# At three seams of a two-layer trunk, lower parts of two token tiles move from GpSimd to VectorE, tanh's table is loaded at the seam, and VectorE's modulation sums are issued behind their unit

## The chip, the cores and the metric

The kernel runs on one core of a Trainium2 chip. The metric is the device time of one execution, in microseconds (us); of several executions the median counts.

The engines are named as the profile names them: PE (TensorE, matmuls) with PEld (its weight loads), DVE (VectorE), ACT (ScalarE), POOL (GpSimd) and SP (SyncE, which issues most DMAs).

## The reference, cut to what matters

Two layers, each a token mixer and a gated FFN with a width-3 depthwise convolution, on 384 tokens (128 context tokens and 256 latent ones) of width 1024. Each half of a layer normalises its input, modulates it by vectors computed from a condition, and adds its normalised, gated output to the residual stream:

```python
D_MODEL, DEPTH, SEQ, DEC_SEQ, D_FF = 1024, 2, 128, 256, 2816

def modulation(cond, w, b):
    m = jax.nn.silu(cond) @ w + b
    return jnp.split(m[..., None, :], 6, axis=-1)

def conv_ffn(h, p):
    gate, up = jnp.split(h @ p['ffn_w_up'], 2, axis=-1)
    gate = dwconv3(gate, p['ffn_conv_w'], p['ffn_conv_b'])
    return (jax.nn.silu(gate) * up) @ p['ffn_w_down']

def trunk_layer(x, mod, p, cache):
    shift1, scale1, gate1, shift2, scale2, gate2 = mod
    h = rms_norm(x, p['norm_g'][0]) * (1.0 + scale1) + shift1
    y, ctx_state = token_mixer(h, p, cache)
    x = x + gate1 * rms_norm(y, p['norm_g'][1])
    h = rms_norm(x, p['norm_g'][2]) * (1.0 + scale2) + shift2
    x = x + gate2 * rms_norm(conv_ffn(h, p), p['norm_g'][3])
    return x, ctx_state
```

Everything is float32.

## The kernel before

**Tiles and products.** The 384 tokens are three tiles of 128 (0, 1, 2). A float32 product is three matmuls: each operand is split into an upper part (a rounding cast) and a lower part (what is left). For weights ACT casts the upper part (`whi`, line 358) and DVE subtracts the lower part (`wlo`, line 359). The input of a projection lies transposed in `hTa` and `hTb` (the two halves of its 1024 columns), each in an upper and a lower part. The upper part is ACT's cast in line 815, the lower part a subtraction in line 818. Line 818 goes to POOL by default, and to DVE in the variants `La` and `Lv`.

**Seams.** Between two halves of a layer stands a seam: for each token tile the post-norm, the residual, the pre-norm, transposes, modulation and split, while PE finishes the last product before and starts the first one behind. The steps of a seam are issued in an order written out by hand, as a string of names; the function `in_order` calls them one by one, and each engine runs its own in that order. There are three such strings that matter here: `OUT_ORDER` (layer 0, mixer to FFN; about 262 to 290 us, called seam A), `FFN_ORDER` (FFN of layer 0 to mixer of layer 1; about 560 to 590 us, seam B) and `OUT_LAST_ORDER` (layer 1, mixer to FFN; about 770 to 798 us, seam C).

A name is a step and a tile number. Those that come up below, `a` and `v` being the halves that ACT and DVE work on:

- `x`: the residual (line 779, DVE); `z`: the normalised tile `xn` (`za` on ACT, line 797; `zv` on DVE, line 795); `t`: its transposes on PE into `tps` (line 802); `h`: the modulation of `tps` into `hf` (`ha` on ACT, line 812; `hv` on DVE, line 810); `i`: the upper part (line 815); `l`: the lower part on POOL, `L` with `a` or `v`: the lower part on DVE (line 818).
- `g`, `u`, `G`, `U`: matmuls of the first FFN unit's gate (`gps`) and up half (`ups`): small letters are the columns of the first two tiles (up to column 258 in layer 0), capitals those behind. `k` is the like for the first projection of layer 1 (`tma`, lines 878 to 880).
- `L` and `A` with a number: load and matmuls of a part of the next layer's modulation (`adaps`, line 407). `W`: eight idle matmuls. `m`: matmuls of the product before the seam.

**The FFN loop.** It runs over 22 units of 128 hidden columns, f = 0 to 21, ordered by a scheduler. A unit is the gate product (24 matmuls of 386 columns into `gps`), a step of the down product (18 matmuls of 512 columns into `facc`, lines 1302 to 1304, for the unit before), and the up product (24 matmuls into `ups`). `gate_act` (line 1311) does the convolution and the activation: line 1315 on ACT, 1316 and 1317 on DVE, tanh in line 1318 on ACT, 1319 on DVE. Line 1562 multiplies by `ups`; the result is split into `fah` (ACT) and `fal` (DVE), the stationary operands of the next unit's down step.

**Modulation sums.** In the FFN of layer 0, half of layer 1's modulation is computed on DVE: `AdaV.rows` (line 501) loads 512 KB blocks into `avr` (two buffers) and adds four products for each pair of blocks into `avc` (lines 503 and 505). The loop advances this by one pair of blocks in unit 3 and in each unit from 6 on. The scheduler puts the sums in DVE's queue where it sees room.

Of the kernel before, what the change touches and what calls it, by code (L numbers as in the profile page):

```python
# [9 lines left out]
F32 = mybir.dt.float32  # L10
# [3 lines left out]
ACTF = mybir.ActivationFunctionType  # L14
ALU = mybir.AluOpType
# [7 lines left out]
TP = 386  # L23
# [245 lines left out]
def trunk(ctx: ExitStack, tc: tile.TileContext, A, O, offs, depth=DEPTH):  # L269
    nc = tc.nc  # L270
    coff0, coff, foff, poff, moff = offs
    V, S, G, T = nc.vector, nc.scalar, nc.gpsimd, nc.tensor
# [211 lines left out]
    class AdaV(Ada):  # L484
# [900 lines left out]
    for l in range(depth):  # L1385
# [147 lines left out]
        with ExitStack() as ph:  # L1533
# [8 lines left out]
            for f in range(NF):  # L1542
# [44 lines left out]
            steps, more = [{} for _ in range(3)], {}  # L1587
# [60 lines left out]
```

## Time and profile before

| | before |
|---|---|
| median of 3 runs | 1080.4 us |
| the three runs | 1078.41, 1080.73, 1080.4 us |
| the profiled execution | 1076.9 us |
| its span | 1075.1 us |
| mean granted TensorE clock | 0.994 |
| PE busy | 1048.2 us, 97% of the span |
| DVE busy | 735.1 us, 68% |
| ACT busy | 512.8 us, 48% |
| POOL busy | 65.9 us, 6% |

The median and the three runs are executions without a profile; the span is the profiled execution's own. The granted clock is a share of full speed, 1.00 being 2.4 GHz and 0.50 being 1.2 GHz. Each row of a timeline gives the start and the length of an instruction in us, its engine and line, what it writes and reads, and in brackets how long its engine stood idle before it and which instruction ended that.

### The profile page before, as it was taken

How to read it: one execution, taken by the hardware profiler on the slowest of the kernel's cores; microseconds unless marked ns; L12 is line 12 of the kernel's file. 1: busy time of each engine (PE TensorE's matmuls, PEld its weight loads, DVE VectorE, ACT ScalarE, POOL GpSimd, SP SyncE). 2: the span in 40 equal slices, each digit the busy share in tenths (PEclk: the TensorE clock that was granted, in tenths of full speed). 3: DMA queues.
4: the chain of work that ended last, by engine and by line, in shares of the span. 5: the costliest groups of instructions: out<-in, count | busy, mean ns of one | idle time of the engine just before them, and what ended most of it. 6: DMA issues, size and time to landing. Idle time of an engine off the chain costs nothing.

```text
span 1075.1 us, 15668 instructions
## 1 busy us (share of the span) xinstructions
PE 1048.2 (97%) x5763; PEld 894.4 (83%) x5763; DVE 735.1 (68%) x1554; ACT 512.8 (48%) x1120; POOL 65.9 (6%) x78
## 2 busy tenths in 40 slices
PE   9999999999889999999998999999999999999997
PEld 3497777768789999989986978977899999999996
DVE  6887875576789984489957677757665455445544
ACT  5765545435744433333446554553674434334333
POOL 3210001000200000000003000101020000000000
PEclk9999999999999999999999999999989999999999
DMA  9774455747557764357656522321545334343301
GB/s 345 238 273 135 154 180 216 289 134 277 179 195 246 235 197 140 121 176 234 209 154 212 196 66 73 98 65 49 207 138 177 118 118 132 127 133 119 121 18 59
DMA packets 53305, 176.05 MB, mean 164 GB/s; under 512 B 8650, under 2 KB 10570, under 8 KB 52973
## 3 DMA queue, kind: packets, MB, share of 16 engines
q1 hardware_dynamic: 49517, 171.19, 47.6%
q10 hardware_dynamic: 3712, 3.87, 1.0%
q8 instruction: 45, 0.74, 0.3%
q14 instruction: 31, 0.25, 0.1%
HBM read 169.60 MB, written 5.44 MB: 163 GB/s over the span
## 4 chain that ended last, share of the span: by engine, by line
PE 86%; DVE 8%; DMA 3%; ACT 2%; issue 1%; POOL 0%; DVEq 0%; SPq 0%; ACTq 0%; POOLq 0%
PE facc L1302 6%; PE facc L1304 6%; PE gps L383 6%; PE facc L1303 6%; PE gps L385 6%; PE gps L384 6%; PE ups L383 5%; PE ups L385 5%; PE ups L384 5%; PE fmps L383 3%; PE fmps L385 3%; PE fmps L384 3%; PE acc L1302 2%; PE acc L1303 2%; PE acc L1304 2%; PE adaps L407 2%
## 5 line engine op out<-in xcount | busy, mean ns | idle before, releaser
L359 DVE TENSOR_TENSOR wlo<-raw,whi 128x512 fp32r<-128x512 f32 (+2 forms) x388 | 254.2, 684 | 162.9 <-ACT whi L358 162.1
L358 ACT CAST whi<-raw 128x512 fp32r<-128x512 f32 (+2 forms) x388 | 221.1, 610 | 260.9 <-DMA raw<-in_wdn_dram 98.1
L1302 PE MATMUL facc<-whi,fah 128*128 128x512 f32 x264 | 105.1, 398 | 2.7 <-ACT fah L358 2.7
L1304 PE MATMUL facc<-whi,fal 128*128 128x512 f32 x264 | 104.8, 398 | 0.0
L1303 PE MATMUL facc<-wlo,fah 128*128 128x512 f32 x264 | 104.5, 396 | 0.0
L505 DVE SCALAR_TENSOR_TENSOR avc<-avr,cs,avc 128x1024 f32<-128x1024 f32 x56 | 70.2, 1280 | 0.2 <-DMA avr<-in_ada_dram 0.2
L383 PE MATMUL gps<-hTa,whi 128*128 128x386 f32 (+4 forms) x184 | 62.4, 339 | 0.2 <-DVE fc L1317 0.2
L383 PE MATMUL gps<-hTb,whi 128*128 128x386 f32 (+4 forms) x184 | 62.2, 338 | 0.0
L383 PE MATMUL ups<-hTa,whi 128*128 128x386 f32 (+4 forms) x184 | 62.2, 338 | 0.0
L383 PE MATMUL ups<-hTb,whi 128*128 128x386 f32 (+4 forms) x184 | 61.6, 335 | 0.6 <-ACT hTb L815 0.6
L384 PE MATMUL ups<-hTb,whi 128*128 128x386 f32 (+4 forms) x184 | 61.4, 334 | 0.8 <-POOL hTb L818 0.8
L385 PE MATMUL gps<-hTa,wlo 128*128 128x386 f32 (+4 forms) x184 | 62.1, 338 | 0.0
L385 PE MATMUL ups<-hTa,wlo 128*128 128x386 f32 (+4 forms) x184 | 61.9, 337 | 0.0
L384 PE MATMUL ups<-hTa,whi 128*128 128x386 f32 (+4 forms) x184 | 61.8, 336 | 0.0
L384 PE MATMUL gps<-hTa,whi 128*128 128x386 f32 (+4 forms) x184 | 61.8, 336 | 0.0
L385 PE MATMUL gps<-hTb,wlo 128*128 128x386 f32 (+4 forms) x184 | 61.7, 335 | 0.0
L384 PE MATMUL gps<-hTb,whi 128*128 128x386 f32 (+4 forms) x184 | 61.7, 335 | 0.0
L385 PE MATMUL ups<-hTb,wlo 128*128 128x386 f32 (+4 forms) x184 | 61.5, 334 | 0.0
L1302 PEld LDWEIGHTS facc<-whi,fah 128*128 128x128 f32 x264 | 49.8, 189 | 13.9 <-ACT fah L358 3.0
L1304 PEld LDWEIGHTS facc<-whi,fal 128*128 128x128 f32 x264 | 50.1, 190 | 12.0
L1303 PEld LDWEIGHTS facc<-wlo,fah 128*128 128x128 f32 x264 | 50.0, 190 | 10.1
L1318 ACT ACTIVATE fth<-fc 128x386 f32<-128x386 f32 x44 | 23.2, 528 | 58.5 <-DVE fc L1317 58.4
(392 smaller groups left out, 2392.6 us busy)
## 6 DMA issues: line engine op xcount, KB each, us to landing
raw<-in_wup_dram SPq DMA_DIRECT2D x88, 512.0 KB, 3.8
araw<-in_ada_dram SPq DMA_DIRECT2D x64, 512.0 KB, 4.5
raw<-in_wdn_dram SPq DMA_DIRECT2D x44, 512.0 KB, 3.8
avr<-in_ada_dram SPq DMA_DIRECT2D x32, 512.0 KB, 4.6
raw<-in_win_dram SPq DMA_DIRECT2D x30, 512.0 KB, 3.9
raw<-in_wout_dram SPq DMA_DIRECT2D x16, 512.0 KB, 3.7
gg<-gd SPq DMA_DIRECT2D x8, 512.0 KB
raw<-in_wta_dram SPq DMA_DIRECT2D x8, 416.0 KB, 3.4
```

The lines of the kernel that those rows point to most:

```text
L358: S.copy(hi, src)
L359: (eng or V).tensor_tensor(out=lo, in0=src, in1=hi, op=ALU.subtract)
L383: T.matmul(out, ah, bh, start=start, stop=False)
L384: T.matmul(out, ah, bl, start=False, stop=False)
L385: T.matmul(out, al, bh, start=False, stop=stop)
L407: T.matmul(self.ps[32 * j:32 * j + 32, :], cs[:, k, :], rows[j // 2][:, 512 * (j % 2):512 * (j % 2) + 512], start=(k == self.k0), stop=(k ...
L505: V.scalar_tensor_tensor(out=acc[:, v, c], in0=raw, scalar=sc, in1=acc[:, v, c], op0=ALU.mult, op1=ALU.add)
L1302: T.matmul(acc[t][h], ah[:, cs_], wh_[:, hs], start=first, stop=False)
L1303: T.matmul(acc[t][h], ah[:, cs_], wl_[:, hs], start=False, stop=False)
L1304: T.matmul(acc[t][h], al[:, cs_], wh_[:, hs], start=False, stop=last)
L1318: S.activation(out=th, in_=c, func=ACTF.Tanh)
```

## The change

1. In `OUT_ORDER` and `OUT_LAST_ORDER` the four lower parts `lv1`, `la1`, `lv2`, `la2` become `Lv1`, `La1`, `Lv2`, `La2`: the same subtraction on DVE. In `FFN_ORDER` the same four move to DVE and to other places: `La1 Lv1` behind `zv2`, and `Lv2 La2` behind `W0`. The lower parts of tile 0 stay on POOL.
2. A new step `th` behind `ia2` in `OUT_ORDER` and `OUT_LAST_ORDER`: a tanh of one column on ACT, which makes ACT load the table of tanh there.
3. `AdaV.rows` issues its sums behind the multiplication of line 1562 of the unit at hand.

```diff
@@ OUT_ORDER, from ia0 on @@
-n2 iv1 L3 ya2 A0 ia0 lv1 ha1 xa2 xb2 sa2 A1 sb2 c2 A2 R2 u0 P2 N2 zv2 g0 ia1 za2 la0 A3 tv2 hv2 ta2 iv2 la1 g1
-ha2 lv2 ia2 W0 u1 U0 hold la2  G0 G1 U1 
+L3 ya2 A0 ia0 Lv1 ha1 xa2 xb2 sa2 A1 sb2 c2 A2 R2 u0 P2 N2 zv2 g0 ia1 za2 la0 A3 tv2 hv2 ta2 iv2 La1 g1 ha2 Lv2
+ia2 th W0 u1 U0 hold La2 G0 G1 U1
@@ OUT_LAST_ORDER, from xa2 on @@
-xa2 lv0 hv1 sa2 c2 R2 W2 P2 ia0 N2 za2 iv1 u0 zv2 ta1 g0 ha1 tv2 ta2 la0 g1 hv2 u1 iv2 lv1 ia1 ha2 lv2 la1 ia2
-la2 G0 W3 U0 U1 G1
+lv0 hv1 sa2 c2 R2 W2 P2 ia0 N2 za2 iv1 u0 zv2 ta1 g0 ha1 tv2 ta2 la0 g1 hv2 u1 iv2 Lv1 ia1 ha2 Lv2 La1 ia2 th
+La2 G0 W3 U0 U1 G1
@@ FFN_ORDER, its end @@
-iv0 yb2 n2 xa2 xb2 lv0 ha1 sa2 sb2 c2 R2 A2 hv1 ia1 P2 iv1 N2 la1 k0 zv2 za2 tv2 ta2 ha2 hv2 iv2 ia2 L3 A3 lv1
- k1 W0 lv2 la2 k2 as
+yb2 n2 xa2 xb2 lv0 ha1 sa2 sb2 c2 R2 A2 hv1 ia1 P2 iv1 N2 k0 zv2 La1 Lv1 za2 tv2 ta2 ha2 hv2 iv2 ia2 L3 A3 k1 W0
+Lv2 La2 k2 as
@@ new function @@
+    def tanh_table():
+        y = sm.tile([128, 1], F32, tag="sqt", name="tht")
+        S.activation(out=y, in_=zero8[:, 0:1], func=ACTF.Tanh)
@@ AdaV.rows @@
-                    for v in range(2):
-                        sc = cs[:, k, v:v + 1]
-                        if k == 0:
-                            V.tensor_scalar(acc[:, v, c], raw, sc, None, ALU.mult)
-                        else:
-                            V.scalar_tensor_tensor(out=acc[:, v, c], in0=raw, scalar=sc, in1=acc[:, v, c], op0=ALU.mult, op1=ALU.add)
+
+                    with tc.issue_after(unit[0].ins):
+                        for v in range(2):
+                            sc = cs[:, k, v:v + 1]
+                            if k == 0:
+                                V.tensor_scalar(acc[:, v, c], raw, sc, None, ALU.mult)
+                            else:
+                                V.scalar_tensor_tensor(out=acc[:, v, c], in0=raw, scalar=sc, in1=acc[:, v, c], op0=ALU.mult,
+                                                       op1=ALU.add)
@@ the seam's steps, and the FFN loop @@
+            more["th"] = tanh_table
...
-                V.tensor_tensor(out=c, in0=pu[:, 0:TP], in1=c, op=ALU.mult)
+                unit[0] = V.tensor_tensor(out=c, in0=pu[:, 0:TP], in1=c, op=ALU.mult)
```

DVE at seam A, before: from the last `yn` (line 774) to the first weight splits of the FFN. Names are what an instruction writes and reads.

```order
L774 TENSOR_TENSOR yn<-acc,gg 128x512
L779 SCALAR_TENSOR_TENSOR x_2653<-yn,rz,x_2653 128x512 x2
...
L795 TENSOR_SCALAR xn<-x_2653,rz 128x512
L810 TENSOR_SCALAR hf<-tps,vec_2209,vec_1947 128x128 x4
L416 COPY sb<-adaps 128x512
L359 TENSOR_TENSOR wlo<-raw,whi 128x512 x6
```

The same place now (line 774 is 781, 779 is 786, 795 is 802, 810 is 817, 818 is 825):

```order
L781 TENSOR_TENSOR yn<-acc,gg 128x512
L825 TENSOR_TENSOR hTb<-hf,hTb 128x4x128
L786 SCALAR_TENSOR_TENSOR x_2653<-yn,rz,x_2653 128x512 x2
...
L802 TENSOR_SCALAR xn<-x_2653,rz 128x512
L817 TENSOR_SCALAR hf<-tps,vec_2209,vec_1947 128x128 x4
L825 TENSOR_TENSOR hTa<-hf,hTa 128x4x128
L825 TENSOR_TENSOR hTb<-hf,hTb 128x4x128
L420 COPY sb<-adaps 128x512
L825 TENSOR_TENSOR hTa<-hf,hTa 128x4x128
L363 TENSOR_TENSOR wlo<-raw,whi 128x512 x6
```

Four subtractions are in DVE's queue that were in POOL's: `Lv1` ahead of tile 2's residual, `La1` and `Lv2` behind the modulation `hv2`, `La2` ahead of the weight splits.

DVE at the start of layer 0's FFN, before: from the gate convolution of unit 0 to the split of its result.

```order
L1316 SCALAR_TENSOR_TENSOR fc<-gps,ffh,fc 128x385
L359 TENSOR_TENSOR wlo<-raw,whi 128x512
L1317 SCALAR_TENSOR_TENSOR fc<-gps,ffh,fc 128x385
L359 TENSOR_TENSOR wlo<-raw,whi 128x512 x3
L503 TENSOR_SCALAR avc<-avr,cs 128x1024
L1319 SCALAR_TENSOR_TENSOR fc<-fth,fc 128x386
L1316 SCALAR_TENSOR_TENSOR fc<-gps,ffh,fc 128x385
L1562 TENSOR_TENSOR fc<-ups,fc 128x386
L1317 SCALAR_TENSOR_TENSOR fc<-gps,ffh,fc 128x385
L359 TENSOR_TENSOR wlo<-raw,whi 128x512
L359 TENSOR_TENSOR fal<-fc,fah 128x386
```

The same place now (1316 is 1323, 1317 is 1324, 1319 is 1326, 1562 is 1571, 359 is 363):

```order
L1323 SCALAR_TENSOR_TENSOR fc<-gps,ffh,fc 128x385
L363 TENSOR_TENSOR wlo<-raw,whi 128x512
L1324 SCALAR_TENSOR_TENSOR fc<-gps,ffh,fc 128x385
L363 TENSOR_TENSOR wlo<-raw,whi 128x512 x2
L1326 SCALAR_TENSOR_TENSOR fc<-fth,fc 128x386
L363 TENSOR_TENSOR wlo<-raw,whi 128x512
L1571 TENSOR_TENSOR fc<-ups,fc 128x386
L363 TENSOR_TENSOR wlo<-raw,whi 128x512
L1323 SCALAR_TENSOR_TENSOR fc<-gps,ffh,fc 128x385
L363 TENSOR_TENSOR fal<-fc,fah 128x386
```

The sum of line 503 is gone from between the weight splits and unit 0's `fc`; the first sums now stand behind line 1571 of unit 3.

PE at the first down step (`facc`), before: the rows ahead of it are the second half of unit 1's up product.

```order
L383 MATMUL ups<-hTb,whi 128x386
L384 MATMUL ups<-hTb,whi 128x386
L385 MATMUL ups<-hTb,wlo 128x386
L383 MATMUL ups<-hTb,whi 128x386
L384 MATMUL ups<-hTb,whi 128x386
L385 MATMUL ups<-hTb,wlo 128x386
L1302 MATMUL facc<-whi,fah 128x512
```

The same place now (383 is 387, 385 is 389, 1302 is 1309):

```order
L387 MATMUL ups<-hTa,whi 128x386
L388 MATMUL ups<-hTa,whi 128x386
L389 MATMUL ups<-hTa,wlo 128x386
L387 MATMUL ups<-hTb,whi 128x386
L1309 MATMUL facc<-whi,fah 128x512
```

The down step begins behind 13 of the 24 matmuls of unit 1's up product, where it began behind 18.

In a later unit of that FFN, DVE ran before:

```order
L505 SCALAR_TENSOR_TENSOR avc<-avr,cs,avc 128x1024
L1319 SCALAR_TENSOR_TENSOR fc<-fth,fc 128x386
L505 SCALAR_TENSOR_TENSOR avc<-avr,cs,avc 128x1024 x2
L359 TENSOR_TENSOR wlo<-raw,whi 128x512 x2
L1562 TENSOR_TENSOR fc<-ups,fc 128x386
L359 TENSOR_TENSOR wlo<-raw,whi 128x512 x2
L359 TENSOR_TENSOR fal<-fc,fah 128x386
L505 SCALAR_TENSOR_TENSOR avc<-avr,cs,avc 128x1024 x2
```

and runs now:

```order
L363 TENSOR_TENSOR wlo<-raw,whi 128x512
L1571 TENSOR_TENSOR fc<-ups,fc 128x386
L511 SCALAR_TENSOR_TENSOR avc<-avr,cs,avc 128x1024
L363 TENSOR_TENSOR fal<-fc,fah 128x386
L511 SCALAR_TENSOR_TENSOR avc<-avr,cs,avc 128x1024 x3
L1323 SCALAR_TENSOR_TENSOR fc<-gps,ffh,fc 128x385
```

The sums of a unit stand together behind its multiplication, one of them ahead of `fal` and three ahead of the next unit's convolution.

## Rows read from the trace of the kernel before

**Rows 1.** The page, busy time of each engine (us, share of span, instructions)

```profile
PE 1048.2 (97%) x5763; PEld 894.4 (83%) x5763; DVE 735.1 (68%) x1554; ACT 512.8 (48%) x1120; POOL 65.9 (6%) x78
```

**Rows 2.** PE's waits over the whole span: what for, us in total, times, longest

```profile
PE tps L802 <- DVE xn L795: 4.5, 3, 2.0
PE facc L1302 <- ACT fah L358: 2.7, 1, 2.7
...
PE ups L384 <- POOL hTb L818: 0.8, 1, 0.8
```

**Rows 3.** Timeline of DVE at seam A

```profile
273.34 2.90 DVE L779 SCALAR_TENSOR_TENSOR x<-yn,rz,x 128x512 f32<-128x512 f32 x2
...
278.19 1.36 DVE L795 TENSOR_SCALAR xn<-x,rz 128x512 f32<-128x512 f32 x1
280.38 1.37 DVE L810 TENSOR_SCALAR hf<-tps,vec,vec 128x128 f32<-128x128 f32 x4 [0.82 <-PE tps L802]
...
296.80 0.75 DVE L503 TENSOR_SCALAR avc<-avr,cs 128x1024 f32<-128x1024 f32 x1 [4.04 <-DMA avr<-in_ada_dram]
...
298.46 0.55 DVE L1562 TENSOR_TENSOR fc<-ups,fc 128x386 f32<-128x386 f32 x1
```

**Rows 4.** Timeline of ACT at seam A

```profile
291.03 1.28 ACT L1318 ACT_TABLE_LOAD   x1 [0.19 <-DVE fc L1317]
...
299.05 0.51 ACT L358 CAST fah<-fc 128x386 fp32r<-128x386 f32 x1 [3.08 <-DVE fc L1562]
```

**Rows 5.** Timeline of POOL at seam A

```profile
274.04 1.65 POOL L818 TENSOR_TENSOR hTa<-hf,hTa 128x512 fp32r<-128x512 f32 x1
278.10 1.18 POOL L818 TENSOR_TENSOR hTa<-hf,hTa 128x512 fp32r<-128x512 f32 x1 [2.40 <-ACT hTa L815]
```

**Rows 6.** Timeline of PE at seam A

```profile
279.61 1.09 PE L802 MATMUL tps<-cst,xn 128*128 128x128 f32 x8 [1.47 <-DVE xn L795]
...
280.66 0.28 PE L384 MATMUL gps<-hTa,whi 128*128 128x258 f32 x1
...
299.62 0.50 PE L1302 MATMUL facc<-whi,fah 128*128 128x512 f32 x1 [2.71 <-ACT fah L358]
```

**Rows 7.** Stretches at seams A and C: busy us by engine, PEclk, DMA

```profile
core 0: us, PE busy (x) PEld busy (x) DVE busy (x) ACT busy (x) POOL busy (x), PEclk, DMA share, GB/s
280.00:284.00 4.00, 4.00 (x41) 3.95 (x39) 1.97 (x5) 2.19 (x6) 1.19 (x1) 1.00 0.00 0
300.00:305.00 5.00, 5.00 (x17) 3.93 (x16) 5.00 (x10) 1.64 (x4) 0.00 (x0) 0.66 0.44 125
785.00:793.00 8.00, 8.00 (x48) 7.95 (x46) 3.99 (x8) 6.89 (x15) 3.99 (x4) 0.57 0.00 0
```

**Rows 8.** Line 818 by engine: duration in ns, shortest, median, longest

```profile
L818 DVE TENSOR_TENSOR hTa<-hf,hTa x2: 676/678/680, 53.3 to 53.9; 128x512 fp32r<-128x512 f32 x2
```

**Rows 9.** Timeline of DVE at seam B

```profile
567.24 0.48 DVE L795 TENSOR_SCALAR xn<-x,rz 128x512 f32<-128x512 f32 x1
...
577.55 1.41 DVE L779 SCALAR_TENSOR_TENSOR x<-yn,rz,x 128x512 f32<-128x512 f32 x2
...
581.05 1.33 DVE L795 TENSOR_SCALAR xn<-x,rz 128x512 f32<-128x512 f32 x1
```

**Rows 10.** Timeline of POOL at seam B

```profile
580.91 1.18 POOL L818 TENSOR_TENSOR hTa<-hf,hTa 128x512 fp32r<-128x512 f32 x1 [3.62 <-ACT hTa L815]
```

**Rows 11.** Timeline of PE at seam B

```profile
582.53 1.06 PE L802 MATMUL tps<-cst,xn 128*128 128x128 f32 x8 [1.06 <-DVE xn L795]
```

**Rows 12.** Timeline of POOL at seam C

```profile
782.88 1.18 POOL L818 TENSOR_TENSOR hTa<-hf,hTa 128x512 fp32r<-128x512 f32 x1 [4.58 <-ACT hTa L815]
```

**Rows 13.** 25 us of layer 0 FFN, columns as in 7

```profile
400.00:425.00 25.00, 25.00 (x132) 23.45 (x132) 12.71 (x22) 9.60 (x19) 0.00 (x0) 1.00 0.49 152
```

**Rows 14.** The page's groups: count, busy us, mean ns of one, idle before

```profile
L505 DVE SCALAR_TENSOR_TENSOR avc<-avr,cs,avc 128x1024 f32<-128x1024 f32 x56 | 70.2, 1280 | 0.2 <-DMA avr<-in_ada_dram 0.2
```

**Rows 15.** The page's DMA issues: count, KB each, median us to landing

```profile
avr<-in_ada_dram SPq DMA_DIRECT2D x32, 512.0 KB, 4.6
```

More of the change, by code (lines that the diff above doesn't have):

```diff
@@ L42 @@
 OUT_ORDER = """
-ma0 ya0 mb0 qa0 qb0 b0 r0 yb0 p0 n0 xa0 xb0 sb0 sa0 ma1 c0 qa1 b1 ya1 mb1 P0 qb1 yb1 p1 R0 r1 n1 L0 xa1 xb1
-sa1 c1 sb1 R1 N0 zv0 P1 ma2 za0 L1 tv0 N1 qa2 b2 mb2 ta0 zv1 za1 hv0 qb2 yb2 tv1 iv0 lv0 r2 p2 hv1 ha0 L2 ta1
-n2 iv1 L3 ya2 A0 ia0 lv1 ha1 xa2 xb2 sa2 A1 sb2 c2 A2 R2 u0 P2 N2 zv2 g0 ia1 za2 la0 A3 tv2 hv2 ta2 iv2 la1 g1
-ha2 lv2 ia2 W0 u1 U0 hold la2  G0 G1 U1
+ma0 ya0 mb0 qa0 qb0 b0 r0 yb0 p0 n0 xa0 xb0 sb0 sa0 ma1 c0 qa1 b1 ya1 mb1 P0 qb1 yb1 p1 R0 r1 n1 L0 xa1 xb1 sa1
+c1 sb1 R1 N0 zv0 P1 ma2 za0 L1 tv0 N1 qa2 b2 mb2 ta0 zv1 za1 hv0 qb2 yb2 tv1 iv0 lv0 r2 p2 hv1 ha0 L2 ta1 n2 iv1
+L3 ya2 A0 ia0 Lv1 ha1 xa2 xb2 sa2 A1 sb2 c2 A2 R2 u0 P2 N2 zv2 g0 ia1 za2 la0 A3 tv2 hv2 ta2 iv2 La1 g1 ha2 Lv2
+ia2 th W0 u1 U0 hold La2 G0 G1 U1
 """
 OUT_LAST_ORDER = """
-ma0 qa0 ya0 mb0 b0 qb0 ma1 r0 p0 n0 yb0 xa0 sa0 xb0 sb0 c0 P0 R0 mb1 qa1 b1 N0 zv0 ya1 qb1 tv0 r1 ma2 yb1 p1
-n1 za0 xa1 xb1 mb2 hv0 sa1 c1 sb1 R1 P1 N1 qa2 iv0 b2 qb2 zv1 tv1 ya2 yb2 r2 W0 za1 p2 ta0 n2 W1 xb2 ha0 sb2
-xa2 lv0 hv1 sa2 c2 R2 W2 P2 ia0 N2 za2 iv1 u0 zv2 ta1 g0 ha1 tv2 ta2 la0 g1 hv2 u1 iv2 lv1 ia1 ha2 lv2 la1 ia2
-la2 G0 W3 U0 U1 G1
+ma0 qa0 ya0 mb0 b0 qb0 ma1 r0 p0 n0 yb0 xa0 sa0 xb0 sb0 c0 P0 R0 mb1 qa1 b1 N0 zv0 ya1 qb1 tv0 r1 ma2 yb1 p1 n1
+za0 xa1 xb1 mb2 hv0 sa1 c1 sb1 R1 P1 N1 qa2 iv0 b2 qb2 zv1 tv1 ya2 yb2 r2 W0 za1 p2 ta0 n2 W1 xb2 ha0 sb2 xa2
+lv0 hv1 sa2 c2 R2 W2 P2 ia0 N2 za2 iv1 u0 zv2 ta1 g0 ha1 tv2 ta2 la0 g1 hv2 u1 iv2 Lv1 ia1 ha2 Lv2 La1 ia2 th
+La2 G0 W3 U0 U1 G1
 """
 FFN_ORDER = """
-ma0 L0 qa0 ya0 mb0 b0 qb0 yb0 ma1 r0 p0 n0 mb1 xa0 sa0 xb0 c0 sb0 ya1 R0 P0 qa1 N0 yb1 qb1 b1 r1 ma2 zv0 za0
-p1 A0 n1 tv0 ta0 mb2 xa1 qa2 sa1 ya2 b2 xb1 hv0 c1 sb1 P1 ha0 L1 R1 N1 A1 ia0 qb2 la0 zv1 tv1 za1 L2 r2 ta1 p2
-iv0 yb2 n2 xa2 xb2 lv0 ha1 sa2 sb2 c2 R2 A2 hv1 ia1 P2 iv1 N2 la1 k0 zv2 za2 tv2 ta2 ha2 hv2 iv2 ia2 L3 A3 lv1
- k1 W0 lv2 la2 k2 as
+ma0 L0 qa0 ya0 mb0 b0 qb0 yb0 ma1 r0 p0 n0 mb1 xa0 sa0 xb0 c0 sb0 ya1 R0 P0 qa1 N0 yb1 qb1 b1 r1 ma2 zv0 za0 p1
+A0 n1 tv0 ta0 mb2 xa1 qa2 sa1 ya2 b2 xb1 hv0 c1 sb1 P1 ha0 L1 R1 N1 A1 ia0 qb2 la0 zv1 tv1 za1 L2 r2 ta1 p2 iv0
+yb2 n2 xa2 xb2 lv0 ha1 sa2 sb2 c2 R2 A2 hv1 ia1 P2 iv1 N2 k0 zv2 La1 Lv1 za2 tv2 ta2 ha2 hv2 iv2 ia2 L3 A3 k1 W0
+Lv2 La2 k2 as
 """
@@ L1327, in trunk @@
     KO = 4
+    unit = [None]
     side = [iter(()), 0]
```

## The prediction

> **What bounds the kernel now.** I read PE's waits first, then each engine's timeline where a wait stands, then the stretches. PE is busy for 97% of the span [rows 1]; in the body of layer 0's FFN it has no gap at all, 25.00 of 25.00 us [rows 13]. So the change can only gain where PE waits, and lose wherever it makes PE wait. PE's waits that bear on it are three for `xn` (4.5 us in all), one of 2.71 us for `fah`, and 0.8 us for `hTb`'s lower part [rows 2]. They stand at the seams.
>
> *Seam A, the 2.71 us.* PE ends its up matmuls at 296.91 and starts `facc` at 299.62, waiting for `fah` [rows 6]. ACT had waited 3.08 us to cast it, for `fc` of line 1562 [rows 4]; that ended on DVE at 299.01, and DVE itself had stood idle for 4.04 us in front of a modulation sum whose `avr` had not landed [rows 3]. So one early sum stands at the head of DVE's queue, and the path's work queues behind it. The clock goes down behind this wait: from 300 to 305 us the granted clock is 0.66 on average [rows 7], between its levels of 2.4 and 1.2 GHz, which costs 5 x (1 - 0.66) = 1.7 us of work.
>
> *The `xn` waits.* DVE's `xn` of line 795 takes 0.48 us when POOL is idle, and 1.33 to 1.36 us when it starts just after a lower part on POOL: at 278.19 behind POOL's 278.10, at 581.05 behind 580.91 [rows 3, 5, 9, 10]. Each time it ends about 0.3 us after POOL's subtraction: DVE waits until POOL is through. PE then waits 1.47 us at 279.61 and 1.06 us at 582.53 [rows 6, 11]. At seam C PE's wait for `xn` is the longest of the three, 2.0 us [rows 2], and there the subtraction that starts just before `xn` is POOL's at 782.88 [rows 12]. By the order this one is `la0`.
>
> **The change part by part.** All against the profiled execution, 1076.9 us (span 1075.1 us), which lies 3.5 us under the median of the runs.
>
> *Seam A, the sum taken away.* DVE has no sum before unit 3. Without it, line 1562 of unit 0 follows tanh (ACT: a table load of 1.28 us from 291.03 and the tanh itself [rows 4]) and not a load, so it ends some 4 us earlier than 299.01. `fah` is then held by what ACT has ahead of it, the casts and the convolution of unit 1: I put it at 296.2 to 296.9 with the delay below included. PE's order now has `facc` 5 matmuls earlier. At 132 matmuls in 25 us [rows 13] that is about 0.9 us, so PE gets there at 296.91 - 0.9 + 0.85 (below) = 296.9. A wait of 0 to 0.3 us stays; I take 0.2. Gain: 2.71 - 0.2 = 2.5 us, and the 1.7 us of clock, if no new wait brings it back: 4.2 us.
>
> *Seam A, the lower parts.* `la1` no longer starts on POOL at 278.10, so `xn` should take 0.48 us and not 1.36: `tps` starts at 278.7 instead of 279.61, and DVE's modulation `hv2` at 279.5 instead of 280.38. But `La1` now stands behind `hv2` on DVE: 279.5 + 1.3 = 280.8, plus 0.68 us for the subtraction on DVE [rows 8], gives 281.5. Before, `la1` was done on POOL at 279.28 [rows 5]. Who waits for it is `g1`, whose second matmul reads that lower part and started at 280.66 [rows 6]. So the 0.9 us that the shorter `xn` gives is lost again, and g1 runs 281.5 - 280.66 = 0.85 us later than before. PE then stands idle for some 1.7 us inside `g1`, instead of 1.47 us before the transposes. All work on PE behind it slips by that 0.85 us. `Lv1` takes 0.68 us on DVE ahead of the residual `x`; POOL's `lv1` is gone from beside that pair, which took 2.90 us there [rows 3]. If nothing hinders, x ends at 273.34 + 0.68 + 1.41 = 275.4, 0.8 us earlier than 276.24 (1.41 us is the same pair at seam B [rows 9]); if the remaining POOL subtraction `la0` (1.65 us at 274.04 [rows 5]) is in the way for 1.2 us, it ends 0.3 us later. I take no change, with these ends for the range. `La2` and `Lv2` stand before weight splits that PE doesn't wait for.
>
> That POOL and DVE can still get into each other's way there is what the row of `x` says, 2.90 us for the pair. The Trainium skill's page "SBUF — State Buffer", section "Who interferes with whom", states more than that row: a DVE instruction with two SBUF inputs contends with a GpSimd one that reads SBUF, and the later of the two stands until the first is through. By that rule `Lv1` itself, a subtraction of two SBUF tiles, meets `la0`, so the moved work can still collide; the sum at seam A would be the lower end just given (0.3 us less gain) and not its middle.
>
> *Seam A, the table.* `th` puts 1.28 us [rows 4] and a tanh of one column on ACT ahead of the first weight casts, and takes the 1.28 us out of `gate_act` of unit 0. The casts slip by 0.6 us or so; PE had no wait for a weight there [rows 2], so I cost it at nothing, with 0.6 us as the bound if that cover is gone. It helps `fah` by making tanh earlier, which is in the 296.2 us above.
>
> Seam A: 4.2 - 0.85 = 3.3 us gained; from 1.0 (the clock not given back and `x` late) to 4.4 (`x` early, no wait left).
>
> *Seam B.* `la1` no longer starts at 580.91 but behind `xn`, so `xn` ends at 581.05 + 0.48 = 581.53 and `tps` starts then and not at 582.53 [rows 11]: PE's wait of 1.06 us goes, gain 1.0 us. `La1` and `Lv1` (2 x 0.68) stand before `hv2`, ending at about 582.8, while `tps` ends at 582.6; `hv2` is 0.2 us late at most, beside matmuls of the next modulation. Those are next to be late: if their weights have not landed by 582.6, PE waits there instead, and the gain is 0.2 us. I take 1.0.
>
> *Seam C.* `la0` stays on POOL, so the wait of 2.0 us and what follows, a granted clock of 0.57 from 785 to 793 [rows 7], or 8 x 0.43 = 3.4 us, have no reason to go. The four moved parts meet an idle DVE. 0, from -0.3 to 0.3.
>
> *Body of layer 0's FFN.* A unit takes half of 25 us, 12.5 us. DVE without sums works 12.71 / 2 = 6.4 us of it [rows 13]; four sums of 1.28 us [rows 14] make 11.5 us, within the unit. Behind line 1562 one sum stands before `fal` and delays it by 1.28 us, to about 2.3 us behind that line; PE has 24 gate matmuls first (4.3 us). The three others delay the next convolution to 5.8 us, where it would start at 4.3; its result is wanted only at 12.5. Cost 0, unless a sum waits for its load (a rival, below). On SP's queue the `avr` loads wait for the buffers of the unit's sums, with later units' weight loads behind them. A buffer comes free 3.4 to 5.8 us into a unit and the load takes 4.6 us [rows 15], so it lands by 8 to 10.4 us, ahead of 12.5.
>
> **Sum:** 3.3 + 1.0 + 0 + 0 = 4.3 us. 1076.9 - 4.3 = 1072.6 for the profiled execution, on the scale of the median 1080.4 - 4.3 = **1076.1 us**. By the ends of the terms it lies between 1.2 and 5.7 us, 1074.7 to 1079.2.
>
> **The rivals.**
> 1. *The new wait inside g1 takes the clock with it.* It is 1.7 us long, and a wait of 2.0 us at seam C was followed by half clock, as was the 2.71 us wait; the 1.47 us wait was not: from 280 to 284 us the granted clock is 1.00 [rows 7]. The price is that of the two cases seen, 1.7 to 3.4 us: the gain falls to 0.9 to 2.6 us, 1077.8 to 1079.5 us.
> 2. *`fah` comes no earlier, since ACT's queue holds it.* ACT's casts ahead of it wait for weight loads and for unit 1's gate product. Then the 2.71 us wait is traded for one of similar length, and only the seam B gain less the 0.85 us is left: 0.2 us, 1080.2 us. Against it: those loads were issued in the same place before.
> 3. *It ends slower: the sums wait for their loads in every unit.* With one sum before `fal`, a late `avr` now holds `fal`, which PE needs about 4.5 us behind line 1562. It decides from the point where `avr` lands later than 4.5 - 1.0 = 3.5 us behind line 1562, that is 16 us behind the last unit's, against 8 to 10.4 us by the medians: weight loads in SP's queue would have to hold it up for 5 us or more. There are 16 units with sums (64 sums by four); at 0.5 us each that is 8 us, less 4.3: slower by 3.7, 1084 us.
> 4. *Seam C gets its clock back too*, because work ahead of it shifts: 3.4 us more, 1072.7 us.
>
> **How the numbers follow.** Forecast 0.52; rival 1 0.18, rival 2 0.12, rival 3 0.11, rival 4 0.07. A measurement of this kernel can tell about 0.2% from no change, 2.2 us: faster means under 1078.2. The forecast is faster but for its upper end (0.05 of the 0.52 goes to no change); rival 1 is faster in half of its cases; rival 4 is faster; rival 2 is no change; rival 3 is slower but for 0.01. Faster: 0.47 + 0.09 + 0.07 = 0.63; the same: 0.05 + 0.09 + 0.12 + 0.01 = 0.27; slower 0.10. The range reaches from rival 4 to rival 2, 1072.5 to 1080.5: out of it lie rival 3 and the edges of the others, together under 0.2.
>
> **What would show it.** Right: no wait for `fah` over 0.5 us near 297 us and full clock from 300 to 305; `xn` at 0.5 us at seams A and B; a new wait of 1 to 2 us in `g1` for DVE's line 818; the wait of 2 us and the low clock still at seam C; PE at 25.00 of 25.00 in the FFN. Wrong: half clock after `g1` (rival 1), a wait of 2 us for `fah` still there (rival 2), gaps on PE in units with sums and DVE idle in front of line 505 (rival 3).

## The result, and the profile after

The changed kernel is slower: 1087.24 us median of 6 runs (1084.46 to 1090.77) against 1079.32 us for the kernel before (6 runs), a ratio of 1.0092 with a 95% interval of 1.0066 to 1.0118. In a second comparison it was 1.0095 (1.0080 to 1.0110). Here and below the ratio is the one on record with the runs; the quotient of the two medians is 1.0073 and lies within its interval. I had forecast 1076.1 us, with 1080.5 us as the upper end.

Seam A went as forecast; the end of layer 0's FFN did not. PE's waits over the whole span of the changed kernel (what for, us in total, times, longest), of which [rows 2] shows those of before:

```profile
PE tps L809 <- DVE xn L802: 8.5, 4, 5.1
...
PE facc L1309 <- ACT fah L362: 1.7, 1, 1.7
PE gps L388 <- DVE hTa L825: 1.7, 1, 1.7
```

There is a wait of 5.1 us for `xn` that was not there, and `facc` still waits for `fah` by name, but in another place. The timeline of PE, at seam A and at the end of layer 0's FFN and seam B:

```profile
283.02 1.09 PE L809 MATMUL tps<-cst,xn 128*128 128x128 f32 x8 [0.62 <-DVE xn L802]
...
285.89 0.36 PE L388 MATMUL gps<-hTa,whi 128*128 128x258 f32 x1 [1.67 <-DVE hTa L825]
...
558.80 0.50 PE L1309 MATMUL facc<-whi,fah 128*128 128x512 f32 x1 [1.74 <-ACT fah L362]
...
579.75 1.12 PE L809 MATMUL tps<-cst,xn 128*128 128x128 f32 x4 [5.07 <-DVE xn L802]
...
594.24 1.06 PE L809 MATMUL tps<-cst,xn 128*128 128x128 f32 x8 [0.83 <-DVE xn L802]
```

At seam A the wait for `xn` is 0.62 us where [rows 6] has 1.47, the wait inside `g1` is the 1.7 us that was forecast, and the 2.71 us wait for `fah` near 300 us is gone. At 558.80 and 579.75 stand 1.74 and 5.07 us of waiting that the kernel before has nowhere. At the gate product of unit 20 (536.50) PE now waits 1.26 us for DVE's `fc`, where it waited 0.17 before (0.33 in a second profile of the changed kernel).

Stretches of the changed kernel (columns as in [rows 7]): seam A, seam B and seam C.

```profile
300.00:305.00 5.00, 4.97 (x24) 3.99 (x23) 4.42 (x8) 2.34 (x5) 0.00 (x0) 1.00 0.88 321
580.00:590.00 10.00, 9.44 (x45) 5.96 (x45) 8.42 (x24) 8.71 (x27) 2.47 (x3) 0.73 0.18 43
797.00:805.00 8.00, 8.00 (x40) 8.00 (x39) 5.10 (x10) 6.85 (x15) 0.00 (x0) 0.50 0.00 1
```

The clock at seam A is full (0.66 before). At seam B it falls to 0.73 on average behind the 5.07 us wait, and at seam C it is down as before ([rows 7] has 0.57).

**Where the time went.** The changed kernel's start minus the start before, at the same piece of work, in the two profiled executions:

| place | before | after | difference |
|---|---|---|---|
| first wait of seam A (`ups`) | 272.98 | 277.35 | +4.4 |
| gate product of unit 2 | 306.51 | 307.59 | +1.1 |
| gate product of unit 19 | 524.7 | 526.6 | +1.9 |
| gate product of unit 20 | 533.5 | 536.5 | +3.0 |
| gate product of unit 21 | 542.1 | 546.1 | +4.0 |
| first `yn` of seam B (DVE) | 560.89 | 572.87 | +12.0 |
| `tps` of tile 1 at seam B | 575.74 | 587.73 | +12.0 |
| `tps` of tile 2 at seam B | 582.53 | 594.24 | +11.7 |
| `tps` of tile 2 at seam C | 784.49 | 796.46 | +12.0 |
| end of the span | 1075.1 | 1088.6 | +13.5 |

Of the 4.4 us ahead of seam A at least 3.4 are not the change's: in a second profile of the changed kernel the first wait of seam A is at 273.95, 1.0 us late. In the first profile 3.6 of them are there by 17 us: seven matmuls of one line (1364, into `wps`) take 3.19 us from 10.63 on, and 1.67 us in the second profile and in the kernel before (line 1356 there). The granted clock is shown as 1.00 in all three, so the reason stays open. From there the change gains 3.3 us at seam A, loses 10.9 us from unit 2 to the first `yn` of seam B, and little else is settled by one profile. In the second profile the same two pieces are -3.6 and +11.6 us. Of the 10.9 us, 0.8 fall into the unit that starts at 461.8 in the changed kernel, 2.2 into units 19 and 20, and 7.9 between the gate product of unit 21 and that `yn`.

**The end of the FFN.** DVE's timeline in the kernel before, from unit 18's multiplication (line 1562) to the first `yn`:

```profile
525.10 0.56 DVE L1562 TENSOR_TENSOR fc<-ups,fc 128x386 f32<-128x386 f32 x1
...
534.96 1.28 DVE L505 SCALAR_TENSOR_TENSOR avc<-avr,cs,avc 128x1024 f32<-128x1024 f32 x1
536.15 0.56 DVE L1562 TENSOR_TENSOR fc<-ups,fc 128x386 f32<-128x386 f32 x1
...
542.47 0.56 DVE L1562 TENSOR_TENSOR fc<-ups,fc 128x386 f32<-128x386 f32 x1
...
550.81 0.56 DVE L1562 TENSOR_TENSOR fc<-ups,fc 128x386 f32<-128x386 f32 x1 [0.42 <-PE ups L385]
...
560.89 1.29 DVE L774 TENSOR_TENSOR yn<-facc,gg 128x512 f32<-128x512 f32 x2 [5.36 <-DMA gg<-gd]
```

and in the changed kernel, the same units (line 1571) and sums (line 511):

```profile
527.24 0.55 DVE L1571 TENSOR_TENSOR fc<-ups,fc 128x386 f32<-128x386 f32 x1
...
538.54 0.55 DVE L1571 TENSOR_TENSOR fc<-ups,fc 128x386 f32<-128x386 f32 x1
539.01 1.27 DVE L511 SCALAR_TENSOR_TENSOR avc<-avr,cs,avc 128x1024 f32<-128x1024 f32 x1
540.21 0.55 DVE L363 TENSOR_TENSOR fal<-fc,fah 128x386 fp32r<-128x386 f32 x1
540.68 3.67 DVE L511 SCALAR_TENSOR_TENSOR avc<-avr,cs,avc 128x1024 f32<-128x1024 f32 x3
...
548.20 0.55 DVE L1571 TENSOR_TENSOR fc<-ups,fc 128x386 f32<-128x386 f32 x1
...
557.65 0.55 DVE L1571 TENSOR_TENSOR fc<-ups,fc 128x386 f32<-128x386 f32 x1
...
559.78 1.28 DVE L511 SCALAR_TENSOR_TENSOR avc<-avr,cs,avc 128x1024 f32<-128x1024 f32 x1
...
572.87 1.29 DVE L781 TENSOR_TENSOR yn<-facc,gg 128x512 f32<-128x512 f32 x2 [6.84 <-DMA gg<-gd]
```

Before, the last sum ends at 536.2 us, ahead of unit 19's multiplication, and the last two units follow each other in 8.3 us. Now every unit to the last has its sums: the last one ends at 561.1 us, and the units follow each other in 9.7 and 9.5 us, with DVE busy without a pause. The loop leaves out the down step for the last three units (the condition `f <= NF - STAG`), so PE's unit is some 8.6 us there (533.5 to 542.1 before) and not 12.7; DVE's 9.6 us no longer fit into it. What these sums make is a row of gates (`gg`): matmuls of PE (into `avps`) use the sums, and the row goes through DRAM (`gd`) and comes back to the first `yn` of seam B. These matmuls before, and the last of them in the changed kernel:

```profile
550.70 1.92 PE L511 MATMUL avps<-avc,one 128*32 128x512 f32 x16
```

```profile
561.59 1.05 PE L518 MATMUL avps<-avc,one 128*32 128x512 f32 x4
```

Before, they run 14 us behind the last sum, where PE's order has them. Now the last of them start 0.5 us behind the last sum. The first `yn` waits for `gg` in both kernels, and comes 12 us later now.

The sums themselves waited for no load. The page's group for them in the changed kernel (count, busy us, mean ns of one, idle before), to set beside [rows 14]:

```profile
L511 DVE SCALAR_TENSOR_TENSOR avc<-avr,cs,avc 128x1024 f32<-128x1024 f32 x56 | 69.3, 1278 | 0.0
```

### The profile page after: what moved, and what is told of

Read it like the earlier page. It is cut to its first block, busy times and chain, and to the rows that moved or that the text cites. A ratio compares the mean times of both kernels' runs of the same rounds, so it can differ in the third digit from the quotient of the medians.

```text
span 1088.6 us, 15670 instructions
## 1 busy us (share of the span) xinstructions
PE 1056.2 (97%) x5763; PEld 897.4 (82%) x5763; DVE 738.1 (68%) x1566; ACT 512.9 (47%) x1122; POOL 51.1 (5%) x66
## 4 chain that ended last, share of the span: by engine, by line
PE 77%; DVE 13%; DMA 4%; ACT 3%; issue 2%; POOL 0%; DVEq 0%; ACTq 0%; SPq 0%; POOLq 0%
PE ups L387 5%; PE gps L387 5%; PE ups L389 5%; PE ups L388 5%; PE gps L388 5%; PE gps L389 5%; PE facc L1309 4%; PE facc L1311 4%; PE facc L1310 4%; PE fmps L387 3%; PE fmps L389 3%; PE fmps L388 3%; DMA raw<-in_wdn_dram 3%; DVE wlo L363 3%; PE adaps L411 2%; PE acc L1309 2%
## 5 line engine op out<-in xcount | busy, mean ns | idle before, releaser
L1311 PEld LDWEIGHTS facc<-whi,fal 128*128 128x128 f32 x264 | 50.0, 190 | 12.7 <-DVE fal L363 0.8
```

Source lines behind the costliest of these rows:

```text
L1311: T.matmul(acc[t][h], al[:, cs_], wh_[:, hs], start=False, stop=last)
```

## The experiments

The theory after the first look: the loss is the tail, that is, the sums that now end behind unit 21 and bring the gate rows late. The rivals: the sums cost in every unit because they stand behind its work; or the lower parts and the table cost the time. All ratios are against runs of the kernel before on the same chip, with 95% intervals.

| kernel | median us | ratio | interval |
|---|---|---|---|
| changed kernel | 1087.2 | 1.0092 | 1.0066 to 1.0118 |
| changed kernel, again | 1087.1 | 1.0095 | 1.0080 to 1.0110 |
| e1_sums_only | 1085.5 | 1.0064 | 1.0041 to 1.0088 |
| e7_tail_only | 1084.2 | 1.0058 | 1.0038 to 1.0077 |
| e2_moves_only | 1081.5 | 1.0023 | 0.9998 to 1.0048 |
| e3_first_only | 1076.6 | 0.9988 | 0.9967 to 1.0009 |
| e4_sooner | 1077.0 | 0.9989 | 0.9970 to 1.0009 |
| e5_la1_first | 1075.5 | 0.9970 | 0.9952 to 0.9988 |
| e6_la0_dve | 1073.6 | 0.9956 | 0.9935 to 0.9977 |
| e8_no_th | 1070.9 | 0.9944 | 0.9927 to 0.9962 |

### Which part loses: e1_sums_only, e2_moves_only, e7_tail_only

e1_sums_only is the changed kernel with the three orders of before (here the end of `OUT_ORDER`):

```diff
-ia2 th W0 u1 U0 hold La2 G0 G1 U1
+ha2 lv2 ia2 W0 u1 U0 hold la2  G0 G1 U1
```

> Only the sums are issued behind their unit; the three seam orders and the table are those of before. Theory (tail): the loss of the changed kernel comes from the sums that now end behind unit 21 of layer 0's FFN, at 561 us, where before they ended behind unit 18, at 536 us: the gate rows that are made from them come back from DRAM 12 us later and PE waits 5 us for xn. Then this kernel must show that loss in full, about +10 us between 525 and 580 us, and the gain at seam A without the wait in g1 (2.7 us of wait and 1.7 us of clock), in sum +6 to +7 us: 1085 to 1087 us. Rival (moves): the lower parts or the table cost the time; then it is 1075 us.

It came out at 1.0064, 1085.5 us: the loss is there without any lower part or table moved. PE's waits at the tail are those of the changed kernel (its timeline of PE):

```profile
553.91 0.50 PE L1309 MATMUL facc<-whi,fah 128*128 128x512 f32 x1 [1.74 <-ACT fah L362]
574.69 1.11 PE L809 MATMUL tps<-cst,xn 128*128 128x128 f32 x4 [4.92 <-DVE xn L802]
```

So the loss does not need the moves. Whether they add to it is not settled: the changed kernel's 1.0092 and 1.0095 lie higher than 1.0064, but the intervals overlap.

e7_tail_only is the kernel before, with the sums of the last three block pairs of the second group alone held back:

```diff
-                    for v in range(2):
+                    with tc.issue_after(unit[0].ins) if self.g == 2 and k >= 5 else nullcontext():
+                        for v in range(2):
```

> The kernel before, with one thing changed: the sums of the last three of the eight block pairs of the second group wait for their units (18 to 21); all others stand where they stood, seam A and the lower parts are as before. It measures the tail by itself. Theory (tail): seam A keeps its 2.7 us wait for fah, and the gate rows come back late: PE waits some 5 us for xn near 570 us; 8 to 11 us slower than before, 1086 to 1089 us. Rival (the loss needs sums behind every unit, since DVE falls behind over the whole FFN): no more than 2 us slower, 1080 us.

It is slower by 0.58%, 6 us. That is more than the rival allows and less than the 8 to 11 us that I expected. Its DVE timeline at the tail (line 1571 of unit 21, the last sum, the first `yn`) and PE's wait for `xn` show why it is less:

```profile
551.01 0.55 DVE L1571 TENSOR_TENSOR fc<-ups,fc 128x386 f32<-128x386 f32 x1
...
553.14 1.28 DVE L511 SCALAR_TENSOR_TENSOR avc<-avr,cs,avc 128x1024 f32<-128x1024 f32 x1
...
564.84 1.29 DVE L781 TENSOR_TENSOR yn<-facc,gg 128x512 f32<-128x512 f32 x2 [5.45 <-DMA gg<-gd]
```

```profile
571.75 1.11 PE L809 MATMUL tps<-cst,xn 128*128 128x128 f32 x4 [3.72 <-DVE xn L802]
```

From the gate product of unit 2 (304.5 here, 306.5 before) to `yn` it loses (564.84 - 560.89) + 2.0 = 6.0 us, as the runs do. Unit 18 has only two sums here, where the changed kernel has four, so DVE enters the short units earlier. Counted from the gate product of unit 2, the last sum ends at 249.9 us here and at 253.5 in the changed kernel, and the first `yn` comes at 260.3 and 265.3. The tail by itself makes about half of the changed kernel's 10.9 us. That the rest comes from holding back the sums ahead of it too is what remains, and no run shows it by itself.

e2_moves_only leaves the sums free and keeps the rest of the change:

```diff
-                    with tc.issue_after(unit[0].ins):
+                    if True:
```

> Only the lower parts and the table; the sums are placed by the scheduler as before. Its order of DVE now has the first sums behind unit 0's multiplication anyway, and the last ones behind unit 18. Theory (tail): no loss, no 5 us wait for xn; the wait for fah at seam A gone or short; 1075 to 1076.5 us, 3 to 4 us under before. Rival (moves): 1085 us or more.

Neither came: 1081.5 us, and the interval holds no change. The tail is indeed gone, and so is the wait for `fah` at seam A. But PE now waits in the middle of the FFN (PE's waits from 300 to 400 us, where the kernel before has none):

```profile
PE facc L1309 <- ACT fah L362: 1.4, 1, 1.4
PE facc L1311 <- DVE fal L363: 0.9, 3, 0.4
```

ACT's timeline shows what `fah` stood behind in the longest of them:

```profile
370.70 2.18 ACT L362 CAST whi<-raw 128x512 fp32r<-128x512 f32 x4 [5.62 <-DMA raw<-in_wdn_dram]
373.15 0.51 ACT L362 CAST fah<-fc 128x386 fp32r<-128x386 f32 x1 [0.27 <-DVE fc L1571]
```

A load of down weights came late, ACT's casts waited for it, and DVE's splits of the same weights stand ahead of `fc`. From unit 2 to unit 19 this profile loses 5.5 us against the kernel before: 2.3 us are these waits, and behind the longest one the granted clock is 0.66 from 375 to 380 us. In this order the scheduler packs five sums behind each of units 3 to 6. That alone can't be the reason, since the kernel before has five or six there and PE doesn't wait. Why the load came late stays open. What the run shows is that a free placement of the sums isn't harmless in every order: e3_first_only, free but for its first pair, has no such wait.

### When the sums end: e3_first_only, e4_sooner

e3_first_only holds back only the first pair of blocks, e4_sooner holds back all but starts units 6 to 9 with more:

```diff
-                    with tc.issue_after(unit[0].ins):
+                    with tc.issue_after(unit[0].ins) if self.g == 0 and k == 0 else nullcontext():
```

```diff
-                    next(nexts, None)
-                    next(nexts, None)
+                    for _ in range(3 if 6 <= f <= 9 else 2):
+                        next(nexts, None)
```

> As the changed kernel, but only the first pair of blocks of the first group waits for its unit (unit 3); all other sums are free. The last sums stand behind unit 18, as before. Theory (tail): the gain at seam A stays (3.3 us), the loss at the tail is gone: 1075 to 1076.5 us. Rival (sums beside every unit delay PE): no statement, since the sums are bunched as before; rival (moves): 1085 us.

> As the changed kernel, all sums behind their unit, but units 6 to 9 take three pieces of the sums and not two, so that the last sums stand behind unit 19 and not 21. It tells whether the loss is in the sums standing behind their unit or in when they end. Theory (tail): the gate rows come two units (17 to 19 us) sooner, ahead of PE's need: no 5 us wait, 1075 to 1078 us. Rival (behind the unit is what costs, by DVE's queue in each unit): 1085 us or more.

Both are as the theory has it, or within 0.1 us of it: 1076.6 and 1077.0 us, ratios of 0.9988 and 0.9989, where the changed kernel has 1.0092. Against the kernel before neither is told from no change, though. e3_first_only kept only 2.0 of the 3.3 us at seam A in its profile (31.5 us from the first wait to the gate product of unit 2), since there the granted clock fell behind the wait in `g1`. Its timeline of PE, and the stretch behind:

```profile
281.07 0.48 PE L388 MATMUL gps<-hTa,whi 128*128 128x258 f32 x1 [1.66 <-DVE hTa L825]
```

```profile
282.00:284.00 2.00, 2.00 (x13) 1.90 (x13) 1.00 (x2) 1.95 (x4) 0.00 (x0) 0.50 0.00 0
```

e4_sooner is the one that decides: its sums stand behind their units as in the changed kernel, and only end two units sooner. Its DVE timeline, the last sum and the first `yn`:

```profile
533.77 1.28 DVE L511 SCALAR_TENSOR_TENSOR avc<-avr,cs,avc 128x1024 f32<-128x1024 f32 x1
...
557.26 0.69 DVE L781 TENSOR_TENSOR yn<-facc,gg 128x512 f32<-128x512 f32 x1 [1.40 <-ACT sqj L753]
```

`yn` no longer waits for `gg` at all, and comes 3.6 us earlier than in the kernel before; 3.0 of them were gained by the gate product of unit 2. PE's wait of 5 us is gone. That shows the loss to lie in when the sums end.

### What is left at seam A: e5_la1_first, e8_no_th

e5_la1_first is e4_sooner with `La1` ahead of `hv2`:

```diff
-za2 la0 A3 tv2 hv2 ta2 iv2 La1 g1 ha2 Lv2
+za2 la0 A3 La1 tv2 hv2 ta2 iv2 g1 ha2 Lv2
```

> As e4_sooner, with La1 of seam A ahead of the modulation hv2 on DVE and not behind it. Theory: DVE is idle there between xn and the transposes for about 0.8 us, so the subtraction (0.6 us) costs nothing and PE's wait of 1.67 us inside g1 goes; from the first wait of seam A to the gate product of unit 2 it takes 28.6 us where the changed kernel took 30.2; 1075 to 1076 us, 1 to 1.7 us under e4_sooner. Rival (hv2 and all behind it only slip, the wait moves to u1): no change against e4_sooner, 1077 us.

The wait inside `g1` went, as expected, but PE gained almost nothing by it: 29.8 us from the first wait of seam A to unit 2's gate product, against 29.9 in e4_sooner (28.6 were expected). The rival named the wrong place (`u1`) but was right in kind. PE comes to `facc` earlier and waits there again for `fah`. The timelines of PE and of ACT:

```profile
297.47 0.50 PE L1309 MATMUL facc<-whi,fah 128*128 128x512 f32 x1 [1.48 <-ACT fah L362]
```

```profile
284.46 1.28 ACT L351 ACT_TABLE_LOAD   x1
...
294.26 1.66 ACT L362 CAST whi<-raw 128x512 fp32r<-128x512 f32 x3 [1.78 <-DMA raw<-in_wdn_dram]
295.83 0.67 ACT L1322 ACTIVATE fc<-gps,ffh 128x386 f32<-128x386 f32 x1
...
296.91 0.51 ACT L362 CAST fah<-fc 128x386 fp32r<-128x386 f32 x1
```

`fah` could be cast from 294.6 on, when DVE had `fc`; it stands behind casts that waited 1.78 us for their weights. SyncE's queue waits for DVE's subtractions (`wlo`) before it issues such loads, 21.9 us in all from 274 to 300 us. These follow ACT's casts of the same weights, and the first casts stand behind `th`.

The runs put e5_la1_first at 0.9970, e4_sooner at 0.9989; the intervals overlap.

e8_no_th is e6_la0_dve (below) without the step `th` at both seams:

```diff
-ia2 th W0 u1 U0 hold La2 G0 G1 U1
+ia2 W0 u1 U0 hold La2 G0 G1 U1
```

> As e6_la0_dve without the step th: tanh's table is loaded in unit 0's activation again, at both mixer-to-FFN seams. Theory (th delays fah): the 1.5 us that th takes on ACT ahead of the first weight casts delays the loads that wait for the casts' buffers, so that later casts wait for the down weights' load (1.3 to 1.8 us) with fah queued behind them; without th, fah comes without PE waiting (1.17 us at seam A and 1.33 us at seam C in e6_la0_dve go), 1071 to 1073 us. Rival (th pays for itself): the table's 1.28 us is back on the path to fah and PE waits as long or longer, 1073.6 to 1076 us.

PE's wait at seam A that went is in e6_la0_dve's list of PE's waits from 284 to 310 us; e8_no_th has none there:

```profile
PE facc L1309 <- ACT fah L362: 1.2, 1, 1.2
```

From the first wait of seam A to unit 2's gate product e8_no_th takes 28.1 us, e6_la0_dve 29.5. The wait at seam C (1.33 us at 797.99) is gone too, but e8_no_th waits 0.6 and 0.4 us two down steps later. In the runs, 0.9944 and 0.9956 can't be told apart. So the step for the table delays `fah` at seam A by about 1.4 us in this arrangement; that it costs the whole kernel anything is not shown.

### POOL's subtraction and DVE's `xn`: e6_la0_dve

e6_la0_dve is e5_la1_first with the lower part of tile 0's first half moved to DVE at seams B and C as well, behind the `xn` that it held up:

```diff
-N1 A1 ia0 qb2 la0 zv1 tv1 za1
+N1 A1 ia0 qb2 zv1 La0 tv1 za1
...
-zv2 ta1 g0 ha1 tv2 ta2 la0 g1 hv2 u1 iv2 Lv1
+zv2 La0 ta1 g0 ha1 tv2 ta2 g1 hv2 u1 iv2 Lv1
```

> As e5_la1_first, with la0 on DVE too at seams B and C, right behind the xn that it held up. Theory (POOL's subtraction holds DVE's xn): xn takes 0.5 us and not 1.4 at both places, PE's waits for it fall from about 1.0 to 0.5 us at B and from 1.96 to 1.1 us at C, and with the shorter wait the clock at C is more often left at full speed (1.4 us at once, 3 to 5 us where half clock is avoided): 1071 to 1074.5 us. Rival (xn waits for something else): 1075 to 1076 us as e5_la1_first, xn still 1.4 us.

It is 0.44% faster than the kernel before (0.23 to 0.65%) and within what was expected. `xn` at seam C takes what it takes alone, PE's wait there falls from 1.97 to 1.08 us, and the clock from 781 to 789 us is full. It is full in e8_no_th's profile too, which has the same short wait. DVE and PE at seam C, and the stretch:

```profile
779.50 0.48 DVE L802 TENSOR_SCALAR xn<-x,rz 128x512 f32<-128x512 f32 x1
```

```profile
780.13 1.06 PE L809 MATMUL tps<-cst,xn 128*128 128x128 f32 x8 [1.08 <-DVE xn L802]
```

```profile
781.00:789.00 8.00, 8.00 (x75) 7.96 (x74) 5.29 (x11) 7.80 (x18) 0.00 (x0) 1.00 0.00 0
```

At seam B `xn` of tile 1 takes 0.49 us too (571.55), and PE's wait before its transposes is gone, but 1.24 us come back at the next one (579.15). What POOL's subtraction did to `xn` is shown; at seam B the time moved on to the next wait.

e8_no_th is the fastest of all, 0.56% under the kernel before (0.38 to 0.73%), 1070.9 us.

### The changed kernel again: a2_changed_again

> The changed kernel once more, for a second profile. Theory: seam A 3.3 us shorter than before, the wait for xn near 580 us some 5 us again, since neither depends on the run; what differs between runs is when the clock reaches full speed in the first 20 us and whether it falls at the seams. 1084 to 1088 us. Rival (the 4.4 us by which the first profile was late at 200 us belong to the change): they are there again.

1087.1 us. Seam A took 29.95 us (30.24 in the first profile, 33.53 before), PE's wait for `xn` was 5.06 us at 576.79, and the 4.4 us ahead of seam A were 1.0 us. So at least 3.4 of them were that execution's. Without these 3.4 us the 13.5 us at the end of the span are 10.1, near what the runs show (0.92% of 1079 us are 9.9).

## Why the prediction was wrong, step by step

**The step that failed** is the body of layer 0's FFN, "four sums of 1.28 us [rows 14] make 11.5 us, within the unit" and, from it, "Cost 0". The numbers in it hold up to unit 18: PE's 25.00 of 25.00 us stayed there but for one stretch (24.45 of 25 us from 457 us on, with a wait of 0.6 us for `avs`), and the offset moved only from +1.1 to +1.9 us up to unit 19's start. They don't hold for the last three units, which have no down step: PE's unit is some 8.6 us there, DVE's 9.6 us. And I asked only whether the sums fit into each unit, not when the last one ends and who waits for that. Before, it ended at 536 us, and the matmuls that use it came at 550.7 us: 14 us of slack. The change moved the last sum by 25 us, to 561.1. That is 10 us past the slack, and through `gd` and `gg` it reached the first `yn`, 12.0 us later. The order of DVE showed where the last sums stand (unit 21 instead of 18) ahead of any run; I quoted a unit from the middle and missed it.

**Rival 3** gave 1084 us and the right sign, but by another mechanism: sums waiting for `avr`. They stood idle for 0.0 us in front of line 511. Its chance of 0.11 can't count as having seen this.

**Seam A** was sized right in sum: 3.3 us forecast, 3.3 and 3.6 us in two profiles. Its terms were right too: the wait for `fah` gone, the clock full from 300 to 305 us, `xn` short, a new wait of 1.67 us in `g1` against 1.7 forecast. The residual `x` ended 3.2 us behind the seam's first wait, 3.3 before, and had been put at no change. Rival 1 did not come in the changed kernel: the clock stayed up behind that wait in both profiles. That was in part luck, since in e3_first_only it fell behind the same wait. What I did not see is that the sums alone bring more: 29.0 us in e1_sums_only against 30.2 in the changed kernel and 33.5 before. So the lower parts and the table together take about 1 us away at seam A. Of that, 0.7 us are PE's waits: 0.71, 0.62 and 1.67 us in the changed kernel, 0.81 and 1.48 in e1_sums_only. The rest is not accounted for. I had put `th` at nothing because PE waits for no weight there, and in the changed kernel PE has no wait that `th` makes. Where the wait in `g1` is gone, `th` does cost time at this seam: not by a wait of PE's for a weight but by ACT's, with `fah` queued behind it (1.48 us in e5_la1_first; about 1.4 us between e6_la0_dve and e8_no_th).

**Seam B**: 1.0 us forecast. `xn` of tile 2 is short (no subtraction of POOL's beside it), but PE's wait went only from 1.06 to 0.83 us, and to 0.51 in the second profile. From tile 1's transposes to tile 2's it took 6.8 us before and 6.5 and 6.2 us after: a gain of 0.3 to 0.6 us. A chain of small DVE steps ahead of `xn` is next to be late. One of them took 1.15 us and not 0.22, and it ends with a lower part of tile 0 that was left on POOL. DVE and POOL:

```profile
588.71 1.15 DVE L767 SCALAR_TENSOR_TENSOR rz<-rz,rb 128x1 f32<-128x1 f32 x1
```

```profile
588.66 1.18 POOL L825 TENSOR_TENSOR hTb<-hf,hTb 128x512 fp32r<-128x512 f32 x1 [1.27 <-ACT hTb L822]
```

Before, this step took 0.59 us, and in e4_sooner 0.59 too; there the two tiles' transposes lie 5.9 us apart and PE waits 0.21 us. So the forecast's 1.0 us nearly came (0.85) once the tail was mended.

**Seam C**: no gain was forecast, and the wait of 1.96 us stayed. The low clock behind it was longer in the first profile (0.50 from 797 to 805 us) and shorter in the second. That is part of the run-to-run spread and not settled.

**The collision of `Lv1` with `la0`**, which the prediction held possible, did take place: `la0` starts on POOL 0.2 us behind `Lv1` and takes 1.51 us (1.18 for others of its kind), and the two `x` behind `Lv1` take 2.33 us (1.41 at seam B). It cost no more than `lv1` and `la0` beside `x` did before, when the two took 2.90 us: `tps` waits 0.6 us, with `xn` at 0.49 us.

**The sum.** Even without the loss at the tail the forecast gain of 4.3 us is not seen in the runs: e4_sooner has 0.9989, at most 0.3% less time. In its profile PE is 3.0 us ahead at unit 2, 2.4 at the end of seam B and at seam C, and 0.9 at the end of the span, behind a longer low clock at seam C (0.50 there, 0.57 before). And the ends of the forecast's range do not follow from its own terms: seam A comes to 1.3 and 4.3 us instead of 1.0 and 4.4, and seam C's 0.3 us stand in the upper end only. The result lies far outside either way.

## What to carry to other kernels

Work that is moved behind something has two ends: check that it fits where it is put, and follow its last instance to whoever uses the result. The end of a loop needs its own look, since an engine's slack there can be another than in the body. And a wait that is taken away on the path can be followed by the next queue's: with `La1` early, PE waited almost as long for `fah` (1.48 us where it had been 1.67).

## What the runs showed of the hardware

The length of a wait on PE does not decide alone whether the clock falls. At seam C the same wait of 1.96 us was followed by a granted clock of 0.50 to 0.81 over 8 us in eight profiles, the kernel before (0.57) and the changed one (0.50) among them, but by full clock in e3_first_only (784 to 792 us):

```profile
784.00:792.00 8.00, 8.00 (x75) 7.96 (x74) 4.74 (x10) 6.92 (x15) 0.00 (x0) 1.00 0.00 0
```

And the 2.33 us wait for `fah` in e7_tail_only left the clock at 1.00 from 300 to 305 us, where 2.71 us took it to 0.66 before. The wait of 1.66 us in `g1` was followed by 0.50 in e3_first_only, as shown above, but by 1.00 in the changed kernel (both profiles), e2_moves_only and e4_sooner. The wait in e7_tail_only and the stretch behind it:

```profile
299.13 0.50 PE L1309 MATMUL facc<-whi,fah 128*128 128x512 f32 x1 [2.33 <-ACT fah L362]
```

```profile
300.00:305.00 5.00, 5.00 (x25) 4.34 (x24) 5.00 (x10) 1.66 (x4) 0.00 (x0) 1.00 0.47 142
```

A forecast should carry such a clock loss as a chance and not as a term.
